# A two-layer hybrid decoder trunk on one core: small opening products and mixer steps queued behind whole projections, band triangles merged, first rows and weights fetched in halves on two queues

## The chip, the core and the metric

The kernel runs on one core of a Trainium2 chip. The metric is the device time of one execution in microseconds. The time before is the median of three runs, 1498.28 us (1497.68 to 1500.63). The profiled execution is a run of its own: it took 1497.97 us, of which the profile's span holds 1496.2 us.

Five engines work from their own instruction lists, each strictly in order: PE (matrix products, with PEld for its weight loads), DVE (vector), ACT (activation), POOL, and SP, which here only issues transfers. A list goes on only when its first instruction has everything that it waits for.

## What is computed

256 rows of 1024 values pass through two layers. Each layer is a half-step feed-forward block (FFN 1), a mixer, and a second feed-forward block (FFN 2). Cut to what matters:

```python
for l in range(DEPTH):                                   # DEPTH = 2
    x = x + 0.5 * rmsnorm(swiglu(rmsnorm(x, g1), w_ffn1_in, w_ffn1_out), ...)
    h = rmsnorm(x, mix_pre_g[l])
    z, xbc, dt, rq, rk, rv, rg, aq, ak, av, gate = split(h @ w_in[l])
    y_ssd = ssd_mixer(z, xbc, dt, ...)                   # chunked scan
    y_ret = retention_mixer(rq, rk, rv, rg, ...)         # chunks of 128
    y_att = swa_sink_attention(aq, ak, av, sinks, band_bias, band_mask)
    y = sum_m(sigmoid(gate_m) * (y_m @ w_branch[m])) @ w_out[l]
    x = x + rmsnorm(y, ...)
    x = x + 0.5 * rmsnorm(swiglu(rmsnorm(x, g2), w_ffn2_in, w_ffn2_out), ...)
```

The attention is causal with a window of 128: a query of the second block of 128 rows sees a triangle of the block before it and the other triangle of its own block, 128 keys in all. There are 16 query heads, 2 key heads, a learned sink per head and a bias that depends on the distance alone.

## The kernel before

All products are made from fp32 values split into a high and a low part (fp32r): `mm3` (L82) issues three matmuls, two on L88 and one on L89, for each slot of 128 input channels. A projection (`gemm`, L96) of one tile t of 128 rows onto 512 columns is 8 slots, 24 matmuls into one PSUM accumulator `acc` (five of these rotate). The FFN out-projection has 22 slots. Weights come as `raw` tiles of 512 KB by SP's queue (`units`, L71; five buffers), are split on ACT (L68, the high part) and DVE (L69, the low part) into `hl`. In the first two chunks of an FFN this is done in halves (128x512).

The rows of x are normalised and transposed by `prenorm` (L173): eight 128x128 transposes on PE (L180), eight scaled copies on ACT (L184, `xT` high), eight on DVE (L188, `xT` low), then two squared sums on ACT (L150). For tile 1 of a stage this is done inside a projection, before slot number `at`.

In an FFN (`ffn`, L336) each projection of a chunk c and a tile t is followed by `swiglu` (L120: Silu on ACT at L125, a product on DVE at L127) and by `transposed` (L155: two transposes of h on PE at L161). In the mixer (`mix`, L739) the key, value and dt columns come first (`kvdt`, 272 columns), followed by `att_kv`, which turns and transposes keys and values (L379, L383). Then eleven projections with their own steps; after each, `pump` (L214) advances the generators of attention, retention and scan by one step each. `finish` runs a generator to its end.

An attention step (`att`, L404) works on four heads and one tile t: scores `pS` on PE (L424), bias and row maximum on DVE (L427), exponentials and the division on ACT (L439, L445), transposes of the probabilities `s` on PE (L451), a copy `pT`, and the product with the values `po` (L459). For t = 1 it keeps 256 score columns per head, of which half are masked, and so has two groups of four transposes.

The order of each engine's list is not the order of the code: a scheduler places the instructions by their dependencies and by the order of the code as priority. `issue_after(i)` in the code adds, for what is written under it, an order behind instruction i on i's own engine; `after` does so for a pair.

The constants of the mixer that no earlier work needs (`mixer_consts`, L727: sink, ea, dsk and dtb as broadcasts of 16 values to 128 partitions, and `cw`, which DVE halves at L737) are placed by the scheduler in the opening of the program, as are the tables of `tables` (L263).

## Time and profile before

| | |
|---|---|
| median of three runs | 1498.28 us |
| the profiled execution | 1497.97 us |
| its span in the profile | 1496.2 us |
| PE busy | 1476.6 us, 99% |
| DVE busy | 996.1 us, 67% |
| ACT busy | 798.4 us, 53% |
| POOL busy | 43.2 us, 3% |
| moved by DMA | 275.28 MB, 184 GB/s in the mean |
| PE in the chain that ended last | 72%, and "issue" 24% |

Busy time of PE holds the pipelined tails of its matmuls, so that one row's end can lie behind the next row's start; the step from one start to the next is what a matmul costs in a full queue. A row of the timeline gives the start, the duration, engine and line, the operation, the tiles, how many equal ones were merged, and in brackets how long the engine stood idle before it and what ended that.

### The profile page before, as it was taken

To read this page: it belongs to the slowest core of one execution; us is meant where nothing else is said; L and a number is where in the kernel's file an instruction comes from. 1 tells how busy PE (TensorE), PEld (TensorE's weight loads), DVE (VectorE), ACT (ScalarE), POOL (GpSimd) and SP (SyncE) were. 2 spreads that over 40 slices of the span, in tenths; PEclk is the share of its full clock that TensorE was granted. 3 is DMA by queue.
4 is the path that set the end of the run, shared out by engine and by line. 5 is a ranking of instruction groups with operands and counts; after the bars stand their busy time and mean duration, and the time that the engine had idled before them with its cause. 6 is when DMAs were issued, how large, how long until landed. Compare 5 with 4: busy or idle time off the path is not lost.

```text
span 1496.2 us, 20006 instructions
## 1 busy us (share of the span) xinstructions
PE 1476.6 (99%) x7277; PEld 1228.2 (82%) x7277; DVE 996.1 (67%) x1647; ACT 798.4 (53%) x1392; POOL 43.2 (3%) x80
## 2 busy tenths in 40 slices
PE   8999999999999999999999999999999999999998
PEld 6888888898888887888878888888888888788886
DVE  6655577688887676655566554777898876755643
ACT  6554466476454456544465454756655544655541
POOL 0000010000100000000000000100001000000000
PEclk9999999999999999999999999999999999999999
DMA  8654456554565545554565544655456645645551
GB/s 302 238 178 169 158 196 208 173 160 152 183 223 185 198 161 194 193 197 153 189 209 186 201 146 172 233 176 163 148 170 200 208 166 176 219 169 173 196 171 66
DMA packets 82771, 275.28 MB, mean 184 GB/s; under 512 B 11120, under 2 KB 15856, under 8 KB 82672
## 3 DMA queue, kind: packets, MB, share of 16 engines
q1 hardware_dynamic: 82384, 273.93, 54.8%
q8 instruction: 57, 0.93, 0.3%
q14 instruction: 42, 0.34, 0.1%
q10 hardware_dynamic: 288, 0.07, 0.0%
HBM read 272.86 MB, written 1.11 MB: 183 GB/s over the span
## 4 chain that ended last, share of the span: by engine, by line
PE 72%; issue 24%; DMA 2%; ACT 1%; POOL 1%; DVE 0%; POOLq 0%; DVEq 0%; ACTq 0%
PE acc L88 39%; PE acc L89 20%; PE xbc L88 3%; PE xbc L89 2%; PE pT L161 1%; PE pS L424 1%; PE py L701 1%; PE po L459 1%; PE pb L451 1%; DMA x<-x 1%; PE po L532 0%; DMA cw<-w_conv 0%; PE pT L180 0%; ACT xT L184 0%; DMA gain<-ffn_post_g 0%
## 5 line engine op out<-in xcount | busy, mean ns | idle before, releaser
L88 PE MATMUL acc<-hl,xT 128*128 128x512 f32 (+1 forms) x2496 | 775.3, 392 | 2.9 <-DVE hl L69 2.9
L69 DVE TENSOR_TENSOR hl<-raw,hl 128x1024 fp32r<-128x1024 f32 (+2 forms) x544 | 592.7, 1108 | 178.5 <-ACT hl L68 160.2
L68 ACT CAST hl<-raw 128x1024 fp32r<-128x1024 f32 (+2 forms) x544 | 510.7, 958 | 239.1 <-PE acc L89 196.3
L88 PEld LDWEIGHTS acc<-hl,xT 128*128 128x128 f32 x2496 | 461.0, 188 | 93.9 <-DVE hl L69 3.6
L89 PE MATMUL acc<-hl,xT 128*128 128x512 f32 (+1 forms) x1248 | 487.2, 392 | 0.0
L89 PEld LDWEIGHTS acc<-hl,xT 128*128 128x128 f32 x1248 | 234.5, 188 | 46.9 <-issue 0.6
L88 PE MATMUL acc<-hl,hT 128*128 128x512 f32 x704 | 216.8, 390 | 0.0
L88 PEld LDWEIGHTS acc<-hl,hT 128*128 128x128 f32 x704 | 131.6, 188 | 26.9
L89 PE MATMUL acc<-hl,hT 128*128 128x512 f32 x352 | 136.4, 389 | 0.0
L127 DVE SCALAR_TENSOR_TENSOR h<-acc,pr,sl 128x256 f32<-128x256 f32 x88 | 42.2, 479 | 119.2 <-ACT sl L125 119.2
L88 PE MATMUL acc<-hl,yT 128*128 128x512 f32 x384 | 120.8, 396 | 0.0
L125 ACT ACTIVATE sl<-acc,pr 128x256 f32<-128x256 f32 x88 | 42.0, 477 | 146.6 <-PE acc L89 146.6
L88 PEld LDWEIGHTS acc<-hl,yT 128*128 128x128 f32 x384 | 71.8, 188 | 16.9 <-issue 2.4
L89 PEld LDWEIGHTS acc<-hl,hT 128*128 128x128 f32 x352 | 66.1, 188 | 13.9
L89 PE MATMUL acc<-hl,yT 128*128 128x512 f32 x192 | 76.1, 396 | 0.0
L88 PE MATMUL xbc<-xT,hl 128*128 128x256 f32 x384 | 72.7, 287 | 0.0
L88 PEld LDWEIGHTS xbc<-xT,hl 128*128 128x128 f32 x384 | 60.4, 191 | 2.2 <-issue 1.5
L166 DVE TENSOR_TENSOR hT<-pT,hT 128x256 fp32r<-128x256 f32 x88 | 37.0, 421 | 30.6 <-ACT hT L164 30.6
L164 ACT CAST hT<-pT 128x256 fp32r<-128x256 f32 x88 | 32.8, 372 | 45.8 <-PE pT L161 45.8
L89 PE MATMUL xbc<-xT,hl 128*128 128x256 f32 x192 | 54.8, 286 | 0.0
L439 ACT ACTIVATE s<-s,nm 128x128 f32<-128x128 f32 (+1 forms) x64 | 28.4, 445 | 34.7 <-DVE nm L433 34.6
L200 DVE TENSOR_TENSOR yg<-acc,gain 128x512 f32<-128x512 f32 x24 | 16.5, 688 | 39.5 <-ACT junk L199 39.5
(189 smaller groups left out, 1149.6 us busy)
## 6 DMA issues: line engine op xcount, KB each, us to landing
raw<-w_ffn_in SPq DMA_DIRECT2D x176, 512.0 KB, 4.8
raw<-w_main SPq DMA_DIRECT2D x152, 512.0 KB, 4.5
raw<-w_ffn_out SPq DMA_DIRECT2D x88, 512.0 KB, 4.6
raw<-w_branch SPq DMA_DIRECT2D x48, 512.0 KB, 4.3
raw<-w_out SPq DMA_DIRECT2D x16, 512.0 KB, 4.5
bias<-rows SPq DMA_DIRECT2D x8, 512.0 KB, 6.3
L<-acs SPq DMA_DIRECT2D x8, 512.0 KB, 5.5
gain<-b_gate SPq DMA_DIRECT2D x6, 512.0 KB, 4.7
```

The costliest lines, as they stand in the source:

```text
L68: nc.scalar.copy(out=hi, in_=src)
L69: nc.vector.tensor_tensor(out=lo, in0=src, in1=hi.bitcast(F32), op=ALU.subtract)
L88: return (mm(ps, xh, wl, start=start, stop=False), mm(ps, xh, wh, start=False, stop=False), mm(ps, xl, wh, start=False, stop=stop))
L89: mm(ps, xl, wh, start=False, stop=stop))
L125: self.last_silu = nc.scalar.activation(out=sl, in_=a, func=AF.Silu, scale=r)
L127: nc.vector.scalar_tensor_tensor(out=h, in0=b, scalar=r, in1=sl, op0=ALU.mult, op1=ALU.mult)
L161: nc.tensor.transpose(ps[:, j], src[:, (q + j) * P:(q + j + 1) * P], self.ident)
L164: nc.scalar.copy(out=d[:, :, 0, ts], in_=p)
L166: nc.vector.tensor_tensor(out=d[:, :, 1, ts], in0=p, in1=d[:, :, 0, ts].bitcast(F32), op=ALU.subtract)
L200: self.nc.vector.tensor_tensor(out=y, in0=ps, in1=g[:, 512 * i:512 * i + 512], op=ALU.mult)
L424: nc.tensor.matmul(pS[:, i, :w], qT[t][:, hb + j + i], kT[:, g, hl, ks], start=hl == 0, stop=hl == 1)
L439: nc.scalar.activation(out=s[:, j], in_=s[:, j], func=AF.Exp, bias=nm[:, j:j + 1], accum_out=l[:, j:j + 1])
```

## The change

Seven edits:

1. In an FFN the two transposes of h of chunks 0 and 1 are held back: they are traced after the next projection and ordered on PE behind its last matmul. In the mixer the same is done for `att_kv` and for `att_q` of the first query projection. The transposes of x for tile 1 move from slot 2 to slot 4 of the second FFN projection, and from slot 5 to slot 7 of the first query projection.
2. `pump` orders what it traces on PE behind the last matmul of the projection before it.
3. Attention for t = 1 keeps 128 score columns per head: a predicated copy on DVE puts the scores of the block before over the masked triangle, the bias is laid out in DRAM as 640 columns per head to match, and the probabilities are transposed once. The values follow as full x v0 + (masked copy) x (v1 - v0), the masked copy `pc` and the difference `vd` being made on DVE.
4. The first rows of x (two halves, SP's queue) and the first weight tile (two halves, ACT's queue) are fetched alternately; the identity is made on POOL instead of fetched.
5. `tables` is ordered on SP behind the last weight fetch issued so far.
6. A Silu of one column on ACT follows the last Tanh of the mixer.
7. A constant `c_prev` is added, `c_ident` dropped.

```diff
     def pump(self):
-        for g in list(self.gens):
-            if next(g, "done") == "done":
-                self.gens.remove(g)
+        with self.tc.issue_after(self.last_mm.ins):
+            for g in list(self.gens):
+                if next(g, "done") == "done":
+                    self.gens.remove(g)
...
         self.x = self.const.tile([P, NT, D], F32, name="x")
-        self.load_x(0)
+        raw = self.rawp.tile([P, 2, 512], F32, tag="raw", name="raw")
+        w = A["w_ffn1_in"][0, 0].rearrange("p (k n) -> p k n", k=2)
+        for i in range(2):
+            nc.sync.dma_start(out=self.x[:, 0, 512 * i:512 * i + 512], in_=A["x"][0, 0:P, 512 * i:512 * i + 512])
+            nc.scalar.dma_start(out=raw[:, i], in_=w[:, i])
+        self.raw0 = raw
...
-        nc.scalar.dma_start(out=ng, in_=A["c_ident"])
+        nc.gpsimd.memset(ng, 1.0)
+        nc.gpsimd.affine_select(out=ng, in_=ng, pattern=[[1, P]], compare_op=ALU.is_equal, fill=0.0, base=0,
+                                channel_multiplier=-1)
...
-        hT, slots = [], {}
+        hT, slots, held = [], {}, []
         order = [(0, 0), (1, 0), (0, 1), (1, 1)] + [(c, t) for c in range(2, NFC) for t in range(NT)]
-        at, where = 2, (1, 0)
+        at, where = 4, (1, 0)
...
             h = self.swiglu(ps[:, 0:256], ps[:, 256:512], r[t])
-            self.transposed(hT[c:c + 1], h, t)
+            if held:
+                with self.tc.issue_after(self.last_mm.ins):
+                    held.pop()()
+            if c < 2:
+                held.append(lambda c=c, h=h, t=t: self.transposed(hT[c:c + 1], h, t))
+            else:
+                self.transposed(hT[c:c + 1], h, t)
             if (c, t) == (2, 1) and self.first:
                 self.first = None
-                self.tables()
+                with self.tc.issue_after(self.fetch.ins):
+                    self.tables()
...
+                    if t:
+                        nc.vector.copy_predicated(out=pS[:, :, :P], data=pS[:, :, P:],
+                                                  mask=self.prev.bitcast(I32).unsqueeze(1).to_broadcast([P, 2, P]))
...
-                pT = []
-                for b in range(t + 1):
-                    pp = self.pbank()
-                    for j in range(4):
-                        nc.tensor.transpose(pp[:, j], s[:, j, b * P:b * P + P], self.ident)
-                    pt = self.t2([4, P], name="pT")
-                    self.copy(pt, pp)
-                    pT.append(pt)
+                pp = self.pbank()
+                for j in range(4):
+                    nc.tensor.transpose(pp[:, j], s[:, j], self.ident)
+                full = self.t2([4, P], name="pT")
+                if t:
+                    nc.scalar.copy(out=full, in_=pp)
+                    cur = self.t2([4, P], name="pc")
+                    nc.vector.tensor_tensor(out=cur, in0=full, in1=self.prev.unsqueeze(1).to_broadcast([P, 4, P]),
+                                            op=ALU.mult)
+                    terms = [(full, vt[:, 0]), (cur, S["vd"])]
+                else:
+                    self.copy(full, pp)
+                    terms = [(full, vt[:, 1])]
...
-            self.att_kv(t, ps)
+            if held:
+                with self.tc.issue_after(self.last_mm.ins):
+                    held.pop()()
+            held.append(lambda: self.att_kv(t, ps))
...
-        main("aq0", 0, s0, 5, self.second)
+        main("aq0", 0, s0, 7, self.second)
...
+        self.after(nc.scalar.activation(out=self.small(1, "w"), in_=self.mhalf, func=AF.Silu), tanh)
```

What the scheduler makes of it is shown at three places. The first is the opening of the program. On DVE there stood before, from the first cast of the identity on (xT is the normalised input, hl the split weights, cw the convolution's weights):

```order
L255 CAST identr<-ng 128x128
L188 SCALAR_TENSOR_TENSOR xT<-pT,pg,xT 128x128 x4
L69 TENSOR_TENSOR hl<-raw,hl 128x512 x2
L188 SCALAR_TENSOR_TENSOR xT<-pT,pg,xT 128x128 x4
L69 TENSOR_TENSOR hl<-raw,hl 128x512 x8
L188 SCALAR_TENSOR_TENSOR xT<-pT,pg,xT 128x128 x8
L69 TENSOR_TENSOR hl<-raw,hl 128x512 x2
L737 TENSOR_SCALAR cw<-cw 128x60
L127 SCALAR_TENSOR_TENSOR h<-acc,pr,sl 128x256
```

and now:

```order
L268 CAST identr<-ng 128x128
L193 SCALAR_TENSOR_TENSOR xT<-pT,pg,xT 128x128 x8
L70 TENSOR_TENSOR hl<-raw,hl 128x512 x8
L770 TENSOR_SCALAR cw<-cw 128x60
L70 TENSOR_TENSOR hl<-raw,hl 128x512 x2
L193 SCALAR_TENSOR_TENSOR xT<-pT,pg,xT 128x128 x8
L70 TENSOR_TENSOR hl<-raw,hl 128x512 x4
L132 SCALAR_TENSOR_TENSOR h<-acc,pr,sl 128x256
```

All eight parts of xT of tile 0 now stand ahead of the first weight split, and cw stands ahead of the low parts of chunk 1's first weights and of tile 1's xT. On ACT, at the same place, before (the first rows issue transfers; junk is the squared sum):

```order
L249 DMA ng<-c_ident 128x128
L303 DMA pg<-ffn_pre_g 128x8
L875 ACT_TABLE_LOAD
L875 ACTIVATE w<-mhalf 128x1
L184 ACTIVATE xT<-pT,pg 128x128 x4
L68 CAST hl<-raw 128x512 x2
L184 ACTIVATE xT<-pT,pg 128x128 x4
L150 ACTIVATE junk,ss<-x 128x512
L68 CAST hl<-raw 128x512 x4
```

and now:

```order
L254 DMA raw<-w_ffn_in 128x512 x2
L319 DMA pg<-ffn_pre_g 128x8
L919 ACT_TABLE_LOAD
L919 ACTIVATE w<-mhalf 128x1
L189 ACTIVATE xT<-pT,pg 128x128 x8
L155 ACTIVATE junk,ss<-x 128x512
L69 CAST hl<-raw 128x512 x6
L155 ACTIVATE junk,ss<-x 128x512
```

The first weight cast moved behind the second four parts of xT and a squared sum, and the gains pg are issued behind two weight halves. The transfers of SP's queue there are now, with nothing of the tables among them:

```order
L253 DMA x<-x 128x512 x2
L79 DMA raw<-w_ffn_in 128x1024 x3
L274 DMA x<-x 128x512 x2
L137 DMA gain<-ffn_post_g 128x1024
L319 DMA pg<-mix_pre_g 128x8
L766 DMA sink<-attn_sinks 128x16
L766 DMA ea<-a_log 128x16
L766 DMA dsk<-d_skip 128x16
L766 DMA dtb<-dt_bias 128x16
L769 DMA cw<-w_conv 128x60
L137 DMA gain<-ret_gn_g 128x1024
```

Between the gain and cw there are only small transfers left; before, c_dmat, c_xi, c_zeta, c_rope and rb stood ahead of the gain, and two weight tiles between the gain and cw.

The second place is PE at the start of FFN 2, behind 30 matmuls of its first two projections before (h is the first product of swiglu, x the rows of tile 1):

```order
L88 MATMUL acc<-hl,xT 128x512 x2
L89 MATMUL acc<-hl,xT 128x512
L161 MATMUL pT<-identr,h 128x128 x2
L180 MATMUL pT<-identr,x 128x128 x8
L88 MATMUL acc<-hl,xT 128x512 x2
```

and now, behind 36 of them, with 12 matmuls between the two kinds of transposes:

```order
L92 MATMUL acc<-hl,xT 128x512
L185 MATMUL pT<-identr,x 128x128 x8
L91 MATMUL acc<-hl,xT 128x512 x2
...
L166 MATMUL pT<-identr,h 128x128 x2
L91 MATMUL acc<-hl,xT 128x512 x4
```

The transposes of h moved behind 18 more matmuls, those of x behind six.

The third place is PE at the last step of attention in a layer (s are the probabilities, pT their transposed copy, po the product with the values, px and rv belong to the scan and to retention). Before, 16 matmuls of the next projection stood between s and po:

```order
L451 MATMUL pb<-identr,s 128x128 x8
L89 MATMUL acc<-hl,xT 128x512
...
L459 MATMUL po<-pT,av 64x256 x4
L650 MATMUL px<-identr,xc 128x128 x4
L532 MATMUL po<-rv,pm 128x256 x2
L88 MATMUL acc<-hl,xT 128x512 x2
```

and now:

```order
L92 MATMUL acc<-hl,xT 128x512
L477 MATMUL pb<-identr,s 128x128 x4
L492 MATMUL po<-pT,av 64x256 x2
L683 MATMUL px<-identr,xc 128x128 x4
L565 MATMUL po<-rv,pm 128x256 x2
L492 MATMUL po<-pc,vd 64x256 x2
L91 MATMUL acc<-hl,xT 128x512 x2
```

The product now stands right behind the transposes whose copy it reads. It is so in both layers at this place; at two others of a layer only a few short products stand between.

More of the change, by code (lines that the diff above doesn't have):

```diff
@@ L74, in units @@
         for h in range(2):
-            raw = self.rawp.tile([P, 2, width], F32, tag="raw", name="raw")
-            nc.sync.dma_start(out=raw, in_=w_ap[2 * u + h].rearrange("p (k n) -> p k n", k=2))
+            raw, self.raw0 = self.raw0, None
+            if raw is None:
+                raw = self.rawp.tile([P, 2, width], F32, tag="raw", name="raw")
+                self.fetch = nc.sync.dma_start(out=raw, in_=w_ap[2 * u + h].rearrange("p (k n) -> p k n", k=2))
             hl = self.hlp.tile([P, 2, 2, width], R, tag="hl", name="hl")
@@ L291, in tables @@
         nc.vector.tensor_tensor(out=rows[:16], in0=ps[:16, :384], in1=nr[:16], op=ALU.add)
-        self.rows = self.dram.tile([16, 384], F32, name="rows")
-        nc.sync.dma_start(out=self.rows, in_=rows[:16])
+        self.rows = self.dram.tile([16, 640], F32, name="rows")
+        nc.sync.dma_start(out=self.rows[:, 0:255], in_=rows[:16, 0:255])
+        nc.sync.dma_start(out=self.rows[:, 384:511], in_=rows[:16, 128:255])
+        nc.sync.dma_start(out=self.rows[:, 511:639], in_=rows[:16, 127:255])
     def const_load(self, n, shape):
@@ L354, in bias_tile @@
         b = self.t4([4, 256], name="bias")
-        src = bass.AP(self.rows.tensor, self.rows.offset + 384 * h0, [[1, P], [384, 4], [1, 256]])
-        self.nc.sync.dma_start(out=b, in_=src)
+        for t in range(NT):
+            src = bass.AP(self.rows.tensor, self.rows.offset + 640 * h0 + 384 * t, [[1, P], [640, 4], [1, P]])
+            self.nc.sync.dma_start(out=b[:, :, t * P:t * P + P], in_=src)
         return b
@@ L408, in att @@
             S["yT2"] = self.new_T(4, "yT")
+            S["vd"] = self.t1([P], name="vd")
+            nc.vector.tensor_tensor(out=S["vd"], in0=vt[:, 1], in1=vt[:, 0], op=ALU.subtract)
         yT = S["yT2"]
@@ L446, in att @@
                 yield
-                pT = []
-                for b in range(t + 1):
-                    pp = self.pbank()
-                    for j in range(4):
-                        nc.tensor.transpose(pp[:, j], s[:, j, b * P:b * P + P], self.ident)
-                    pt = self.t2([4, P], name="pT")
-                    self.copy(pt, pp)
-                    pT.append(pt)
+                pp = self.pbank()
[11 more added lines that the diff above has]
+                    terms = [(full, vt[:, 1])]
                 yield
                 po = self.pst.tile([P, 2, P], F32, tag="pst", name="po")
-                for b in range(t + 1):
+                for b, (p, v) in enumerate(terms):
                     for o in range(2):
-                        nc.tensor.matmul(po[64 * o:64 * o + 64], vt[:, vo + b, 64 * g:64 * g + 64],
-                                         pT[b][:, o::2], start=b == 0, stop=b == t)
+                        nc.tensor.matmul(po[64 * o:64 * o + 64], v[:, 64 * g:64 * g + 64], p[:, o::2],
+                                         start=b == 0, stop=b == t)
                 y = yT[h0 // 4]
@@ L763, in kvdt @@
                                            op0=ALU.mult, op1=ALU.add)
-            self.att_kv(t, ps)
+            if held:
+                with self.tc.issue_after(self.last_mm.ins):
+                    held.pop()()
+            held.append(lambda: self.att_kv(t, ps))
+        held = []
         def main(key, t, slots, at=None, do=None):
@@ L768, in main @@
             n = int(key[2]) if len(key) > 2 else 0
-            if key[:2] == "aq":
+            if held:
+                with self.tc.issue_after(self.last_mm.ins):
+                    held.pop()()
+            if key == "aq0":
+                held.append(lambda: self.att_q(n, t, ps))
+            elif key[:2] == "aq":
                 self.att_q(n, t, ps)
@@ L836, in mix @@
                                                    op0=ALU.mult, op1=ALU.add)
-                    nc.scalar.activation(out=g, in_=g, func=AF.Tanh, scale=0.5)
+                    tanh = nc.scalar.activation(out=g, in_=g, func=AF.Tanh, scale=0.5)
                     self.pump()
@@ L920, in host @@
     out.update(consts())
-    out["c_ident"] = np.eye(P, dtype=np.float32)
     return out
```

12 lines of the change are left out of this document (8 added, 4 removed).

## The prediction

> **What bounds the kernel now.** I read the head of the page first: who is busy.
>
> ```profile
> PE 1476.6 (99%) x7277; PEld 1228.2 (82%) x7277; DVE 996.1 (67%) x1647; ACT 798.4 (53%) x1392; POOL 43.2 (3%) x80
> ```
>
> PE is the bound from end to end. So only two things can shorten the run: matmuls that are not issued, and idle time of PE. Work that moves on DVE or ACT, which are idle for a third and nearly half of the span, counts only where PE comes to wait for it. The next view is therefore the waits of PE alone (us in total, times, longest):
>
> ```profile
> PE pT L161 <- DVE h L127: 6.0, 3, 2.4
> PE acc L88 <- DVE hl L69: 2.9, 1, 2.9
> PE pb L379 <- ACT kh L370: 2.8, 2, 1.4
> PE acc L254 <- DVE warm L251: 1.4, 1, 1.4
> ```
>
> These are all: 13.1 us in seven waits, and no wait at all in the attention, retention and scan steps. The last row is the program's start and stays. The other three are what the change goes for.
>
> **The held products.** Around the longest wait, at the start of FFN 2 of the first layer, the timeline has:
>
> ```profile
> 566.96 0.39 PE L89 MATMUL acc<-hl,xT 128*128 128x512 f32 x1
> 567.63 0.39 PE L89 MATMUL acc<-hl,xT 128*128 128x512 f32 x1
> 568.10 1.28 ACT L125 ACT_TABLE_LOAD   x1 [3.14 <-PE acc L89]
> 569.40 0.47 ACT L125 ACTIVATE sl<-acc,pr 128x256 f32<-128x256 f32 x1
> 569.91 0.49 DVE L127 SCALAR_TENSOR_TENSOR h<-acc,pr,sl 128x256 f32<-128x256 f32 x1 [2.45 <-ACT sl L125]
> 570.45 0.44 PE L161 MATMUL pT<-identr,h 128*128 128x128 f32 x2 [2.42 <-DVE h L127]
> ```
>
> PE's list holds the transposes of h right behind the projection that h comes from, so PE waits out a table load, a Silu and a product. Three matmuls lie between the first two rows, so one is 0.23 us. In the new order 18 more matmuls and the transposes of x stand between, about 5 us, against the 2.42 us of the wait. What is late next would be xT of tile 1, but 12 matmuls follow the transposes of x before it is read: some 2.7 us, and its first part needs one group of ACT copies (1.14 us) and one DVE part behind it. The early Silu takes the table load (1.28 us) to a place where ACT waits anyway; it is worth nothing beyond this, since the wait is already covered. I take the whole 6.0 us; ends are 0 (next paragraphs' rival) and 6.0.
>
> The same at the start of the mixer:
>
> ```profile
> 204.58 1.42 DVE L209 SCALAR_TENSOR_TENSOR x<-yg,r,x 128x512 f32<-128x512 f32 x2 [1.43 <-POOL r L143]
> 205.14 0.39 PE L89 MATMUL acc<-hl,xT 128*128 128x512 f32 x1
> 206.23 0.63 ACT L370 ACTIVATE kh<-acc,pr 128x128 fp32r<-128x128 f32 x2 [3.81 <-DVE dtx L762]
> 206.91 0.33 PE L379 MATMUL pb<-revr,kh 128*128 128x128 f32 x1 [1.38 <-ACT kh L370]
> ```
>
> PE gets six matmuls (1.4 us) and then the transposes of x, whose input is there at 206.0, in place of the wait for kh, which is there at 206.9. Both layers: 2.8 us less. The transposes that follow are now close to the next projection, but the first part of xT's high half stands about 1.3 us behind its transposes, and PE still has three matmuls and four short products (1.1 us) ahead of it; what is left, 0.2 us, I neglect.
>
> **The merged triangles.** Attention for t = 1 issues one group of four transposes where it had two. Four such steps run in each of two layers, so 8 x 4 = 32 transposes go; the products with the values stay the same number. In a full queue eight of them take (a row of the chain):
>
> ```profile
> 286.27 0.87 PE pb L451 x8
> ```
>
> so 0.109 us each and 3.5 us in all, off PE directly. DVE gets 16 predicated copies, 8 products and 2 differences, and loses half the width of 32 reductions; at no more than 0.69 us each (the row of a 128x512 DVE operation below) it is under 18 us on an engine that idles for 500. It costs nothing while the steps keep PE covered.
>
> **Steps behind whole projections.** This is the part with a price. Before, a step's products on PE stood where their inputs were long ready; now at three places of a layer the product with the values follows the transposes of its probabilities at once, or with 0.8 us of other products between. What has to happen in between is one copy:
>
> ```profile
> L68 ACT CAST hl<-raw 128x1024 fp32r<-128x1024 f32 (+2 forms) x544 | 510.7, 958 | 239.1 <-PE acc L89 196.3
> L232 ACT COPY pT<-pb 128x512 f32<-128x512 f32 x12 | 7.0, 585 | 0.8 <-PE pb L451 0.8
> L69 DVE TENSOR_TENSOR hl<-raw,hl 128x512 fp32r<-128x512 f32 x112 | 70.7, 686 | 44.6 <-ACT hl L68 43.8
> ```
>
> A last transpose ends about 0.25 us after its start, the copy takes 0.585 us and a hand-over some 0.05 us on either side: 0.9 us. With nothing between, that is 0.9 us of idle PE; with 0.8 us between, 0.1 us; and where the masked copy on DVE (0.69 us by the third row) comes behind it, about 0.3 us more at one place. 1.4 us a layer, 2.8 us in all. The lower end is 0. The upper end: at each of the six places the copy stands behind a weight cast on ACT, 0.96 us each by the first row, so 2.8 + 5.8 = 8.6 us. I take 2.8, since ACT is busy only half of the time.
>
> **The opening.** Here the trace speaks against the change. The rows:
>
> ```profile
> 4.59 1.38 PE L180 MATMUL pT<-identr,x 128*128 128x128 f32 x8
> 5.57 1.14 ACT L184 ACTIVATE xT<-pT,pg 128x128 fp32r<-128x128 f32 x4 [2.44 <-PE pT L180]
> 7.50 1.14 ACT L68 CAST hl<-raw 128x512 fp32r<-128x512 f32 x2 [0.79 <-DMA raw<-w_ffn_in]
> 8.15 1.29 DVE L69 TENSOR_TENSOR hl<-raw,hl 128x512 fp32r<-128x512 f32 x2 [0.28 <-ACT hl L68]
> 8.90 1.22 PE L88 MATMUL acc<-hl,xT 128*128 128x512 f32 x2 [2.93 <-DVE hl L69]
> 9.56 0.64 ACT L150 ACTIVATE junk<-x 128x512 bf16<-128x512 f32 x1
> 10.08 0.21 ACT L150 ACTIVATION_READ_ACCUMULATOR junk<-x 128x1 f32 x1
> 15.05 2.17 ACT L184 ACTIVATE xT<-pT,pg 128x128 fp32r<-128x128 f32 x8
> 16.93 1.07 PE L88 MATMUL acc<-hl,xT 128*128 128x512 f32 x4
> ```
>
> The first matmul waits for the first weights, which land at 7.5 us. With halves they land earlier, but that is not what PE will wait for: ACT's new list has all eight parts of xT (2.17 us) and one squared sum (0.64 + 0.21 us) ahead of the first weight cast (0.57 us), and DVE's low part (0.64 us) comes behind that. And xT needs the gains pg, which are now issued behind two weight halves on ACT's queue. The windows of the opening (two last columns: share of the DMA engines' time, GB/s; before them the granted clock of PE):
>
> ```profile
> 2.00:4.00 2.00, 2.00 (x6) 1.58 (x5) 0.00 (x0) 1.12 (x2) 0.00 (x0) 1.00 0.83 282
> 4.00:6.00 2.00, 1.97 (x10) 1.39 (x9) 0.23 (x1) 0.43 (x2) 0.00 (x0) 1.00 0.92 249
> 8.00:10.00 2.00, 1.10 (x3) 0.91 (x4) 1.58 (x4) 2.00 (x7) 0.00 (x0) 0.67 1.02 412
> 10.00:12.00 2.00, 2.00 (x6) 1.33 (x5) 2.00 (x6) 2.00 (x6) 0.00 (x0) 0.50 1.06 413
> 12.00:14.00 2.00, 2.00 (x10) 1.55 (x10) 1.81 (x4) 2.00 (x5) 0.84 (x2) 0.97 1.04 383
> ```
>
> The four halves are 1.05 MB; the first 6 us moved 1.06 MB, so pg is there at about 6.2 us and no earlier than 5.57. The first matmul then starts at 6.2 + 2.17 + 0.85 + 0.57 + 0.64 + 0.2 for hand-overs = 10.6 us, 1.7 later than now (1.1 later with pg at 5.57).
>
> The clock columns say that PE ran at half clock for about 3.5 us after its idle 2.9 us. The gap grows to some 5 us, so I keep these 3.5 us as they are. The Trainium skill, TensorE: Matmul & The Clock Gate, "What's actually happening", says that the clock drops after an idle window of about 3.4 us and comes back after as long a busy one; by it the sum would be the same, unless the gap were cut short, which is part of the first rival. The Trainium skill, DMA: Bandwidth & Descriptors, "Issuing engines are not separate DMA queues", says that transfers issued by several engines share the same 16 DMA engines and interleave; the share of 1.02 to 1.06 at 412 GB/s agrees, and by it the two queues bring the sum of the four halves no earlier.
>
> A second thing decides the opening, and comes later. The new list of DVE holds cw ahead of the low parts of chunk 1's first weights and of xT of tile 1. Before, these stood ahead of it. The chain has:
>
> ```profile
> 12.04 5.18 DMA gain<-ffn_post_g
> 17.24 6.57 DMA cw<-w_conv
> ```
>
> so the gain landed at 17.22 us and cw at 23.81 us, 6.59 us later, with two weight tiles and five small transfers between (DVE even waited 3.06 us for it, at no cost to PE). Ahead of the gain there go now:
>
> ```profile
> c_dmat<-c_dmat SPq DMA_DIRECT2D x1, 256.0 KB, 8.7
> c_xi<-c_xi SPq DMA_DIRECT2D x1, 256.0 KB, 7.9
> c_rope<-c_rope SPq DMA_DIRECT2D x1, 192.0 KB, 5.8
> ng<-c_ident ACTq DMA_DIRECT2D x1, 64.0 KB, 3.4
> ```
>
> 768 KB, 1.9 us at 412 GB/s: the gain lands at 15.3 us. Two weight tiles of 512 KB are 2.5 us, so the small transfers cost 6.59 - 2.5 = 4.1 us, and cw lands at 19.4 us. DVE then needs about 0.2 us for cw and 0.64 us for the first low part, and PE can start its 27th matmul (chunk 1 with tile 0) at 20.3 us. Now, PE starts its 25th at 16.93 us and its 27th 0.46 us later, at 17.4. So PE is 2.9 us late here. From the first matmul alone it would be 1.7 us late; the two do not add, the later one counts. Ends: 1.1 us, if cw is early and pg as now; and with the four broadcasts twice as slow, 2.9 + 4.1 = 7.0 us. Weights are no bound behind this: 34 matmuls (7.8 us) of chunk 0 and of what has landed stand ahead of the next tile's.
>
> POOL's fill and selection for the identity have no row of their own; a mean POOL instruction takes 43.2 / 80 = 0.54 us, and from the program's start to the transposes at 4.59 us two of them have room for four times that. I take nothing; were they slower than this, the opening would move by the excess, one for one, and no reason speaks for a gain.
>
> **The sum.** -6.0 - 2.8 - 3.5 + 2.8 + 2.9 = -6.6 us on the profiled execution's 1497.97, so 1491.4; the median of the runs is 0.3 us above that execution, so 1491.7 us for the median.
>
> **Rivals.** First, the opening gains as its edits say: the first matmul no longer waits (2.9 us), and neither cw nor pg is late. Then -6.0 - 2.8 - 3.5 + 2.8 - 2.9 = -12.4 us, 1485.9 us. For it: the weights do land first at 7.5 us. Against it: the order of ACT and DVE above. 0.15.
>
> Second, cw is the later end: the opening loses 7.0 us, the sum is -2.5 us, and the time 1495.8, hardly measurable. For it: the chain ran through cw even before. Half of the way to it is as likely as the end itself. 0.12.
>
> Third, the waits only move: the held products wait where they are now (their inputs come later too, because steps bunch on DVE), and only the transposes are saved. -3.5 + 2.8 + 2.9 = +2.2 us: 1500.5 us, no change. Against it: 5 us of cover against 2.42. 0.08.
>
> Fourth, on the other side: slower. With each step's products bunched behind a projection, PE waits at most pumps and not at six places, for a copy of the kind above with no cover, 0.9 us. A layer has about 20 pumps between the first attention step and the last; 40 x 0.9 = 36 us in place of 2.8, so +26.6 us and 1524.9 us. It decides from 14 such waits on: 14 x 0.9 = 12.6 us against the 9.4 us that the rest gains and the 3 us that can be measured. For it: DVE is the busiest helper in these stretches, and five accumulators give it only so much lag. Against it: in the new order only three places of a layer have so little cover. 0.05.
>
> The forecast itself gets 0.60. A difference of 0.2%, 3 us, is about what a measurement of this kernel can tell from no change. Below 1495.3 lie the forecast, the first rival and half of the second: 0.60 + 0.15 + 0.06 = 0.81; within 0.2% the other half of the second and the third, 0.14; slower the fourth, 0.05. The range holds the forecast with the bounds of its two unknown costs on the steps and in the opening, not both at their worst, and reaches to the first two rivals: 1485.0 to 1497.0 us.
>
> **What would show it.** In the new profile: no wait of PE for h or kh; 64 transposes in the group of s in place of 96; the first matmul of a projection at 10 to 11 us, behind a squared sum on ACT; DVE idle before cw until about 19 us, and PE idle until about 20; waits of PE for pT at three places of a layer, a microsecond or less each. I am wrong in the opening if the first matmul stands before 8.9 us or the 27th before 17.4; wrong on the steps if PE's waits for copies exceed 8.6 us; wrong on the gain if the rows for h or kh are still there.

## The result and the profile after

The changed kernel takes 1507.86 us (median of four runs, 1507.58 to 1508.1), the kernel before 1498.93 us (four runs). The ratio is 1.0059, 95% interval 1.0041 to 1.0076: slower by about 9 us. The prediction was 1491.7 us with a range up to 1497.0; it had the wrong sign and missed by 16 us. Of all executions timed here one, of own_slots below, ran slow (2599.94 us at a mean granted clock of 0.67); without it the median of that run is 1489.93 us and not 1489.98.

The profiled execution took 1508.1 us, its span is 1506.4 us, 10.2 more than before. The busy row of PE and the waits of PE (engine, line, what it waited for: us in total, times, longest) answer to the first two views of the prediction:

```profile
PE 1480.7 (98%) x7245; PEld 1228.7 (82%) x7245; DVE 993.8 (66%) x1665; ACT 792.5 (53%) x1394; POOL 42.2 (3%) x82
```

```profile
PE acc L91 <- DVE hl L70: 5.6, 1, 5.6
PE po L492 <- DVE pc L482: 4.2, 2, 2.1
PE acc L91 <- DVE gz L595: 3.2, 2, 1.8
PE pb L477 <- ACT s L473: 1.8, 3, 0.8
PE acc L91 <- DVE rv L821: 1.7, 2, 0.8
PE acc L267 <- DVE warm L264: 1.5, 1, 1.5
PE po L492 <- ACT pT L480: 1.3, 2, 0.7
```

The rows for h and kh are gone, as forecast. In their place stand five rows of the mixer, 12.2 us. PE's busy time rose by 4.1 us though it has 32 matmuls fewer: part of them ran at half clock.

Where the time went is read by setting the start of the same product on PE side by side in the two traces (us). Edit 1 moves the transposes of x against the matmuls around them, so the start of a mixer is read behind them, at a matmul of the query projection of tile 1 (L89 before, L92 now) ahead of which both lists hold the same products:

| product on PE | before | after | after - before |
|---|---|---|---|
| first of the out-projection of FFN 1, layer 0 | 137.87 | 141.27 | +3.40 |
| in the query projection of tile 1, mixer 0 | 228.16 | 229.78 | +1.62 |
| first of the second branch, layer 0 | 466.23 | 475.84 | +9.61 |
| first of the out-projection of FFN 2, layer 0 | 689.57 | 696.55 | +6.98 |
| first of the out-projection of FFN 1, layer 1 | 877.84 | 883.45 | +5.61 |
| in the query projection of tile 1, mixer 1 | 968.12 | 971.97 | +3.85 |
| first of the second branch, layer 1 | 1206.14 | 1219.20 | +13.06 |
| first of the out-projection of FFN 2, layer 1 | 1429.54 | 1439.91 | +10.37 |

So the opening cost 3.4 us; the held transposes of h gave 2.6 + 1.4 + 2.7 = 6.7 us back (the early Silu lies in the same stretches); each start of a mixer gave 1.8 us; and the stretch from there to the second branch cost 8.0 us in the first layer and 9.2 us in the second. The last two numbers are the surprise.

The opening in the timeline of the changed kernel:

```profile
8.47 2.18 ACT L189 ACTIVATE xT<-pT,pg 128x128 fp32r<-128x128 f32 x8 [4.78 <-DMA pg<-ffn_pre_g]
...
11.10 3.25 ACT L69 CAST hl<-raw 128x512 fp32r<-128x512 f32 x6
...
12.54 1.22 PE L91 MATMUL acc<-hl,xT 128*128 128x512 f32 x2 [5.62 <-DVE hl L70]
...
16.73 0.19 DVE L770 TENSOR_SCALAR cw<-cw 128x60 f32<-128x60 f32 x1
```

The order of ACT is the one that the prediction showed; but pg lands at 8.4 us, not 6.2, so the first projection starts at 12.54 us and not at 10.6. cw has no idle time in brackets: nothing waited for it.

The end of attention in the first layer, in the timeline of the changed kernel (ACT, DVE and PE):

```profile
340.57 0.59 ACT L238 COPY pT<-pb 128x512 f32<-128x512 f32 x1 [1.21 <-PE pb L477]
341.06 0.69 ACT L594 ACTIVATE gz<-acc,rh 128x512 f32<-128x512 f32 x1
...
360.61 0.59 ACT L480 COPY pT<-pb 128x512 f32<-128x512 f32 x1 [0.30 <-PE pb L477]
...
361.15 2.36 DVE L70 TENSOR_TENSOR hl<-raw,hl 128x1024 fp32r<-128x1024 f32 x2
...
362.04 0.69 ACT L594 ACTIVATE gz<-acc,rh 128x512 f32<-128x512 f32 x1
...
363.82 0.69 DVE L482 TENSOR_TENSOR pc<-pT,c_prev 128x512 f32<-128x512 f32 x1
364.56 1.12 PE L492 MATMUL po<-pc,vd 128*64 128x256 f32 x4 [2.08 <-DVE pc L482]
366.29 0.68 DVE L595 SCALAR_TENSOR_TENSOR gz<-gz,acc 128x512 f32<-128x512 f32 x1
367.03 1.22 PE L91 MATMUL acc<-hl,xT 128*128 128x512 f32 x2 [1.34 <-DVE gz L595]
```

gz (`silu2`, L590 of the changed kernel) is what reads a gate projection out of its accumulator, first on ACT (L594), then on DVE (L595). There is one for each tile of 128 rows. On ACT the first runs at 341 us, the second 21 us later, each close behind a copy pT of an attention step. PE first waits for the masked copy pc, and then for the accumulator that the second gz still holds. The same stretch of the timeline before has the two together:

```profile
343.12 0.59 ACT L232 COPY pT<-pb 128x512 f32<-128x512 f32 x1 [0.21 <-PE pb L451]
343.61 1.27 ACT L561 ACTIVATE gz<-acc,rh 128x512 f32<-128x512 f32 x2
```

And the waits bring the clock down. The windows of PE there (window, PE busy and instructions, granted clock, share of the DMA engines, GB/s):

```profile
361.00:364.00 3.00, 1.48 (x9) 1.00 0.69 209
364.00:367.00 3.00, 1.12 (x4) 0.58 0.87 288
367.00:370.00 3.00, 2.97 (x7) 0.50 0.64 195
370.00:373.00 3.00, 3.00 (x12) 0.78 0.02 7
```

From 367.03 to about 371.3 us PE runs at half clock, which costs 2.1 us, and 0.5 us more on the four products at 364.56 (1.12 us in place of 0.65). In the second layer, by the same rows, it is 2.8 us. Waits of 12.2 us and 5.4 us of half clock are 17.6 us, against the 17.2 us by which the two stretches grew.

### The profile page after: what moved, and what is told of

Same layout as the page of the kernel before. It is cut to its first block, busy times and chain, and to the rows that moved or that the text cites. A ratio compares the mean times of both kernels' runs of the same rounds, so it can differ in the third digit from the quotient of the medians.

```text
span 1506.4 us, 20004 instructions
## 1 busy us (share of the span) xinstructions
PE 1480.7 (98%) x7245; PEld 1228.7 (82%) x7245; DVE 993.8 (66%) x1665; ACT 792.5 (53%) x1394; POOL 42.2 (3%) x82
## 4 chain that ended last, share of the span: by engine, by line
PE 85%; issue 12%; DVE 1%; ACT 0%; DMA 0%; POOL 0%; ACTq 0%; DVEq 0%; POOLq 0%
PE acc L91 48%; PE acc L92 24%; PE xbc L91 3%; PE pT L166 2%; PE xbc L92 2%; PE pS L449 1%; PE py L734 1%; PE po L492 1%; PE pT L185 1%; PE pb L477 1%; DVE hl L70 0%; DMA pg<-ffn_pre_g 0%; PE po L565 0%; PE pb L422 0%; PE px L683 0%
## 5 line engine op out<-in xcount | busy, mean ns | idle before, releaser
L91 PE MATMUL acc<-hl,xT 128*128 128x512 f32 (+1 forms) x2496 | 778.0, 393 | 10.4 <-DVE hl L70 5.6
L92 PE MATMUL acc<-hl,xT 128*128 128x512 f32 (+1 forms) x1248 | 488.9, 393 | 0.0
L92 PEld LDWEIGHTS acc<-hl,xT 128*128 128x128 f32 x1248 | 235.6, 189 | 47.2 <-issue 0.6
L92 PE MATMUL acc<-hl,hT 128*128 128x512 f32 x352 | 136.4, 389 | 0.0
L91 PEld LDWEIGHTS acc<-hl,yT 128*128 128x128 f32 x384 | 71.8, 188 | 17.1 <-issue 2.9
L92 PEld LDWEIGHTS acc<-hl,hT 128*128 128x128 f32 x352 | 66.1, 188 | 13.8
L92 PE MATMUL acc<-hl,yT 128*128 128x512 f32 x192 | 75.7, 394 | 0.0
L92 PE MATMUL xbc<-xT,hl 128*128 128x256 f32 x192 | 54.6, 285 | 0.0
L92 PEld LDWEIGHTS acc<-hl,yT 128*128 128x128 f32 x192 | 36.1, 188 | 7.3
```

Source lines behind the costliest of these rows:

```text
L91: return (mm(ps, xh, wl, start=start, stop=False), mm(ps, xh, wh, start=False, stop=False), mm(ps, xl, wh, start=False, stop=stop))
L92: mm(ps, xl, wh, start=False, stop=stop))
```

## The experiments

Each was timed in five rounds beside the kernel before (its medians were 1500.4 to 1501.0 us in these groups). The changed kernel was not timed again there, so a difference to its 1507.86 us is one between groups, in which the kernel before lay 1.5 to 2.1 us apart. The table has all runs; the ratio is to the kernel before, with its 95% interval. Edits 5 and 6 were not undone by themselves, and what each is worth stays open.

| run | median us | ratio |
|---|---|---|
| bands_apart | 1506.19 | 1.0039 (1.0027 to 1.0052) |
| mix_unheld | 1492.34 | 0.9950 (0.9937 to 0.9962) |
| unheld_apart | 1495.13 | 0.9966 (0.9952 to 0.9979) |
| old_fetch | 1504.84 | 1.0028 (1.0017 to 1.0039) |
| q_now | 1491.16 | 0.9938 (0.9924 to 0.9952) |
| kv_now | 1508.74 | 1.0056 (1.0042 to 1.0069) |
| unheld_old_fetch | 1490.36 | 0.9932 (0.9919 to 0.9945) |
| pg_first | 1504.97 | 1.0027 (1.0015 to 1.0038) |
| catch_up | 1507.29 | 1.0045 (1.0031 to 1.0060) |
| late_start | 1493.31 | 0.9955 (0.9942 to 0.9968) |
| pc_pool | 1506.22 | 1.0041 (1.0028 to 1.0054) |
| q_now_old_fetch | 1488.23 | 0.9921 (0.9907 to 0.9936) |
| own_slots | 1489.98 | 0.9928 (0.9916 to 0.9940) |
| own_catch_up | 1497.36 | 0.9977 (0.9968 to 0.9985) |
| own_old_fetch | 1487.37 | 0.9913 (0.9900 to 0.9927) |
| own_q_now_old_fetch | 1486.59 | 0.9909 (0.9895 to 0.9923) |

One suspect needed no run. With the `issue_after` in `pump` (edit 2) taken out, the lists of all five engines come out the same, instruction by instruction. And with all the other edits undone and edit 2 kept, the lists are those of the kernel before. Edit 2 moves nothing; what the prediction put down to it is the work of another edit.

**Which edit: the merge or the held products?** Two edits, undone one by one and together.

bands_apart puts `bias_tile`, `rows` and `att` back as they were:

```diff
-                pp = self.pbank()
-                for j in range(4):
-                    nc.tensor.transpose(pp[:, j], s[:, j], self.ident)
+                for b in range(t + 1):
+                    pp = self.pbank()
+                    for j in range(4):
+                        nc.tensor.transpose(pp[:, j], s[:, j, b * P:b * P + P], self.ident)
```

> The changed kernel with edit 3 undone: attention for t = 1 again keeps 256 columns, two groups of transposes, no masked copy pc. Held products and all else stay. Theory H (the held products of the mixer push attention one projection later, so that its last steps stand with little cover between transposes and product, whatever the products are): the transposes come back (+3.5 us), the waits for pc go (4.2 us and what follows on them, at most 8 us), waits for pT of the other kind come in their place; 1503 to 1511 us. Theory M (the masked copy on DVE and the added DVE work of the merge cost the time, in any order): 1507.9 + 3.5 - 18.7 = 1492.7 us, and no PE waits for pT above 1 us in all.

mix_unheld leaves the merge and undoes the mixer's part of edit 1:

```diff
-            held.append(lambda: self.att_kv(t, ps))
+            self.att_kv(t, ps)
...
-            if key == "aq0":
-                held.append(lambda: self.att_q(n, t, ps))
-            elif key[:2] == "aq":
+            if key[:2] == "aq":
...
-        main("aq0", 0, s0, 7, self.second)
+        main("aq0", 0, s0, 5, self.second)
```

> The changed kernel with the mixer's part of edit 1 undone: att_kv and att_q are traced at once again, the transposes of x stand before slot 5 of the first query projection. The merge of the triangles and the held transposes of the FFNs stay. Theory H: between the transposes of s and the product that reads their copy there are 3.5 us of other matmuls or more, so no PE waits for po, s, gz, rv; kh waits return (at most 2.8 us): 1507.9 - 18.7 + 1.5 to 2.8 = 1490.7 to 1492 us. Theory M: pc still stands behind weight splits on DVE, PE waits for it: 1505 to 1510 us.

unheld_apart has both diffs.

> Both undone: the mixer's held products and the merge. What stays of the change are the opening, the held transposes of the FFNs, the early Silu, the order of the tables. Theory H: mix_unheld plus 32 transposes of 0.109 us: 1494 to 1495.5 us. Theory M: the same as bands_apart, 1492.7 us or a little above by the waits for kh. Against the kernel before both say: + 3.4 (opening) - 6.7 (waits for h) = -3.3 us.

Without the merge: 1506.19 us. Without the held products: 1492.34 us. The waits of PE in mix_unheld are

```profile
PE acc L91 <- DVE hl L70: 5.7, 1, 5.7
PE pb L403 <- ACT kh L394: 2.8, 2, 1.4
PE acc L267 <- DVE warm L264: 1.5, 1, 1.5
```

and nothing else of note: no pc, gz, s or rv. The masked copy is there in the same number, on the same engine, and PE never waits for it. Theory M falls; the loss belongs to the held products of the mixer. unheld_apart at 1495.13 shows what the merge is worth: 2.8 us in the medians, of which 1.1 us are a difference of the two openings in the traces, so nearer to 2. Beside the held products it is worth nothing: bands_apart, without the merge, took 1506.19 us and the changed kernel 1507.86.

**Which held product?** q_now and kv_now each undo one half.

```diff
-            if key == "aq0":
-                held.append(lambda: self.att_q(n, t, ps))
-            elif key[:2] == "aq":
+            if key[:2] == "aq":
```

> The changed kernel with one thing of edit 1 undone: att_q of the first query projection is traced at once; att_kv stays held, the transposes of x stay before slot 7. Theory Hq (holding att_q lets attention start one pump later, so that its last steps meet the end of the projections; this is the cost): one place per layer with no cover between transposes and product is left, 0.74 us each, the others go and with them the half clock; no kh wait either: 1490.5 to 1492.5 us. Theory Hkv (holding att_kv, which makes keys and values late, is the cost) or slot 7: it stays at 1505 to 1510 us.

```diff
-            if held:
-                with self.tc.issue_after(self.last_mm.ins):
-                    held.pop()()
-            held.append(lambda: self.att_kv(t, ps))
+            self.att_kv(t, ps)
```

> The reverse: att_kv is traced at once, att_q of the first query projection stays held, slot 7 stays. Theory Hq: all waits at the end of attention stay (pc 2.1 us, gz 1.7 us, s 0.8 us, rv 0.8 us a layer and the half clock), and waits for kh can come back: 1507.5 to 1510 us. Theory Hkv: 1491 to 1494 us.

1491.16 and 1508.74 us: holding att_q is the whole of it. In q_now one wait of the five is left,

```profile
PE po L492 <- ACT pT L480: 1.4, 2, 0.7
```

the one place where the product stands right behind its transposes, and it costs what the prediction had worked out for such a place (0.7 us against 0.9).

**Why? First answer: attention is one pump late.** With att_q held, the first attention generator finds its queries one projection later. catch_up gives the step back; late_start makes q_now late in the same way.

```diff
+            if key == "aq1" and not t:
+                next(att[0])
             self.pump()
```

> The changed kernel, att_q still held, and one step of attention more: at the pump behind the first aq1 projection the first attention generator is advanced twice, so that it is level with the kernel in which att_q is not held. Theory Hq (the one pump that attention starts late is the cost): the waits for pc, gz, s and rv go, one wait of 0.7 us for pT per layer stays, 1490.5 to 1492.5 us. If the held products themselves (their place on PE, or what they delay on DVE and ACT) cost it: 1505 to 1510 us.

```diff
         while f"aq{g}1" not in S:
             yield "wait"
+        if g == 0:
+            yield "wait"
```

> The kernel with att_q traced at once (q_now), but the first attention generator lets one pump pass before its first step. The last steps then have 2.2 to 4.8 us of other matmuls between transposes and product, not 0.0 to 1.0 as in the changed kernel. If a late start alone brings the loss: 1503 to 1510 us. If the loss needs the little cover that the last steps have in the changed kernel's list: PE waits for gz or pc for less than 3 us in all, 1490.5 to 1495 us.

Both went against it. catch_up stayed at 1507.29 us; its waits at the end of attention are gone but for 1.3 us for pT, but PE now waits earlier, about 265 to 290 us, for rb, the rotation's second tile:

```profile
PE acc L91 <- DVE rb L512: 5.0, 2, 2.5
PE xbc L91 <- DVE rb L512: 4.8, 3, 2.5
```

late_start took 1493.31 us, 2 us more than q_now, with small waits:

```profile
PE po L494 <- DVE pc L484: 1.4, 2, 0.7
PE pb L479 <- ACT s L475: 0.7, 2, 0.3
```

Lateness alone is worth 2 us. The theory falls; the other answer that late_start allowed, that the loss needs the little cover of the changed kernel's last steps, stands so far.

**Is it DVE's list?** pc stands behind two weight splits of 1.2 us each on DVE. pc_pool moves it to POOL.

```diff
-                    nc.vector.tensor_tensor(out=cur, in0=full, in1=self.prev.unsqueeze(1).to_broadcast([P, 4, P]),
+                    nc.gpsimd.tensor_tensor(out=cur, in0=full, in1=self.prev.unsqueeze(1).to_broadcast([P, 4, P]),
```

> The changed kernel with the masked copy pc made by POOL, which is idle there, and not by DVE. Theory Q (PE waits because pc stands behind two weight splits in DVE's list): the wait for pc goes or falls under 0.5 us a layer, and with it the clock's drop; 1500 to 1503 us. Theory B (the whole list of DVE is late there, pc only the first that PE meets): PE then waits for gz, which frees the accumulator, until about the same time; DVE has 0.7 us less to do at each place, 1505.5 to 1507.5 us.

1506.22 us. The wait for pc fell from 4.2 to 2.6 us, and the wait for gz grew from 3.2 to 6.6:

```profile
PE acc L91 <- DVE gz L595: 6.6, 2, 3.3
...
PE po L492 <- POOL pc L482: 2.6, 2, 1.3
```

pc is only the first late thing that PE meets. Behind it stands the accumulator that gz has not emptied. Theory B has the number right, and its reason, that the whole list of DVE is late there, is part of it: in the changed kernel gz is late on ACT first (362.04 us), though ACT is idle for 47% of the span, and its second half on DVE comes another 4.3 us later (366.29 us), at the end of a stretch in which DVE has not waited since 357.87 us.

**What gz waits for: a buffer.** gz, rb, pT and pc are all tiles of `t2`, one set of ten buffers. In the compiled program of both kernels all 139 tiles of t2 are first written in the order of the code, without one exception. So gz of tile 1, which the code has behind an attention step, should get no buffer before that step's pT and pc have theirs, and these come only when the step's transposes are done. Until then the projection's accumulator stays full, and PE has five of them. own_slots gives pT and pc three buffers of their own and leaves seven to t2; nothing else of the code is touched.

```diff
-N4, N2, N1 = 17, 10, 6
+N4, N2, N1 = 17, 7, 6
...
-                full = self.t2([4, P], name="pT")
+                full = self.big.tile([P, 4, P], F32, tag="pp", name="pT", bufs=3)
...
-                    cur = self.t2([4, P], name="pc")
+                    cur = self.big.tile([P, 4, P], F32, tag="pp", name="pc", bufs=3)
```

> The changed kernel, all edits kept, but the transposed probabilities pT and their masked copy pc have three buffers of their own; the shared buffers t2 go from ten to seven. Theory F (buffers of t2 are given out in the order of the code: the tanh of a gate projection, gz, can't have one before the attention step written ahead of it has had its own for pT and pc, so an accumulator stays full until the step's transposes are done; with att_q held the steps are late and this falls on rg0 of tile 1): gz of tile 1 stands right behind that of tile 0 on ACT, no PE wait for gz, pc under 1 us a layer, 1490 to 1495 us. Theory L (the steps of attention are late and DVE has too much to do at the end, whatever the buffers): 1503 to 1510 us.

1489.98 us: 17.9 us less than the changed kernel (19.7 us by the two ratios), with every edit kept and the same memory. These are all waits of PE that are left:

```profile
PE acc L91 <- DVE hl L70: 5.8, 1, 5.8
PE acc L267 <- DVE warm L264: 1.5, 1, 1.5
```

and on ACT gz no longer stands behind a pT:

```profile
329.61 0.67 ACT L594 ACTIVATE gz<-acc,rh 128x512 f32<-128x512 f32 x1
...
334.77 0.59 ACT L238 COPY pT<-pb 128x512 f32<-128x512 f32 x1 [0.20 <-PE pb L477]
...
340.06 0.67 ACT L594 ACTIVATE gz<-acc,rh 128x512 f32<-128x512 f32 x1
```

The first gz runs 11.5 us earlier than in the changed kernel, the second 22 us earlier. That the two would stand together, as expected, did not come true: they run about 4 and 9 us behind the last matmuls of their projections, where it was about 16 and 31 us, and the second one's half on DVE follows 1.6 us behind its half on ACT, not 4.3. Theory L falls: the crowd on DVE goes with the shared buffers. One thing is not separated by this run. The lists of PE, ACT and DVE come out in another order with it, and the products of the layer's last two steps now start 5.4 and 6.5 us behind their last transpose, where in the changed kernel they start 1.5 and 1.0 us behind it. So the shared set is shown as the cause of the loss; how much of it went because the accumulators come free, and how much because the last products have cover again, is not shown. Nor was one larger shared set tried. The same buffers in catch_up:

> The kernel with att_q held and one step of attention more (catch_up, 1507.3 us, in which PE waited 9.8 us for rb of the rotation), with the same buffers of their own for pT and pc. Theory F: rb took its buffer behind pT of a step ahead of it in the code; the waits for rb go, 1490 to 1494 us. If the extra step crowds DVE there whatever the buffers: 1503 to 1508 us.

1497.36 us: 10 us better, but 3 us short of the expectation. The waits at the end stay away; 7.0 us of waits for rb remain in six places (9.8 in five without). Whether seven shared buffers are too few there or the extra step crowds DVE wasn't tried and stays open.

**The opening.** old_fetch undoes edit 4 alone; pg_first keeps it and only issues the gains ahead of the weight halves on ACT's queue.

```diff
-        for i in range(2):
-            nc.sync.dma_start(out=self.x[:, 0, 512 * i:512 * i + 512], in_=A["x"][0, 0:P, 512 * i:512 * i + 512])
-            nc.scalar.dma_start(out=raw[:, i], in_=w[:, i])
-        self.raw0 = raw
+        self.load_x(0)
+        self.raw0 = None
...
-        nc.gpsimd.memset(ng, 1.0)
-        nc.gpsimd.affine_select(out=ng, in_=ng, pattern=[[1, P]], compare_op=ALU.is_equal, fill=0.0, base=0,
-                                channel_multiplier=-1)
+        nc.scalar.dma_start(out=ng, in_=A["c_ident"])
```

> The changed kernel with edit 4 undone: x and the first weight tile are fetched whole tile by tile on SP's queue, the identity comes by DMA on ACT's queue ahead of the gains pg. Everything behind the opening keeps its order on PE. If the opening's loss comes from pg (issued behind two weight halves, landing at 8.4 us) and its half clock, the first projection's matmul is back at about 8.9 us and the time is 1507.9 - 3.4 = 1504.5 us. If cw ahead of the low parts decides the opening, as the prediction had it, PE still waits there at about 17 to 20 us and the time stays within 1 us of 1507.9.

```diff
+        self.pg0 = self.sm.tile([P, KD], F32, tag="pg", name="pg", bufs=2)
+        nc.scalar.dma_start(out=self.pg0, in_=A["ffn1_pre_g"][0])
         for i in range(2):
```

> The changed kernel with the gains pg issued on ACT's queue ahead of the two weight halves and not behind them; the list of ACT then has four parts of xT, four weight casts and only then the other four parts. PE's list is the same but for two rows. Theory P (the opening lost by pg, which landed at 8.4 us behind a whole weight tile): pg lands by 3 us, xT starts at about 5.7 us, weights are there at 5.2 and 6.4 us, the first matmul of a projection starts at 8.0 to 8.5 us, and 1507.9 - 4 = 1504 us. Theory C (cw ahead of the low parts decides, as the prediction had it): the first matmul is early but PE idles later, 1506 to 1508 us.

1504.84 and 1504.97 us: 3 us each by the medians (3.4 and 4.3 us by the spans of the traces), and as much by moving one transfer of 4 KB as by undoing the whole edit. The DMA issues (KB each, us from issue to landing) of pg in the changed kernel and in pg_first:

```profile
pg<-ffn_pre_g ACTq DMA_DIRECT2D x1, 4.0 KB, 6.7
```

```profile
pg<-ffn_pre_g ACTq DMA_DIRECT2D x1, 4.0 KB, 3.5
```

It landed at 8.4 us there and at 4.2 us here, later than the 3 us expected. In pg_first the first projection starts at 8.71 us, 0.2 us before the kernel before; it then waits once more, since the second weight half lands only at 8.3 us, and runs at half clock:

```profile
8.71 0.74 PE L91 MATMUL acc<-hl,xT 128*128 128x512 f32 x2 [2.14 <-DVE hl L70]
...
10.51 1.14 PE L91 MATMUL acc<-hl,xT 128*128 128x512 f32 x2 [0.83 <-DVE hl L70]
```

cw lands at 18.7 us in it, and between 18 and 20 us PE waits 0.4 us for a low part that stands behind cw on DVE: theory C fits pg_first in small, and the changed kernel not at all.

**The versions that beat both.**

> The mixer's part of edit 1 and edit 4 undone together: merge, held transposes of the FFNs, early Silu and the order of the tables stay. If the two costs are apart in time and add: 1492.3 - 3.0 = 1489.3 us. If the opening's loss is made up later (PE runs into the same late thing in both): 1491 to 1492.3 us.

> The version that the runs so far point to: of the changed kernel everything but the holding of att_q and the fetches in halves (edit 4). q_now took 1491.2 us and the old fetches gave 2 us beside the unheld mixer and 3 us alone: 1488.2 to 1489.2 us, faster than both kernels; at 1491 or above the two gains would not add.

> own_slots with the fetches of before (edit 4 undone). Theory F: 3 us below own_slots, 1487 to 1492 us: with buffers of their own all of the held products can stay. Theory L: 1500 to 1507 us.

> q_now_old_fetch (1488.2 us), the best so far, with the buffers of their own: between transposes and product there are now 3 us of other matmuls or more everywhere, so the wait for pT of 0.7 us a layer goes: 1486.5 to 1487.5 us; if seven shared buffers are too few for the rest, slower than 1488.2.

They took 1490.36, 1488.23, 1487.37 and 1486.59 us; the second and the last as expected, the first 1 us above (the old fetches gave 2.0 us there and not 3.0), own_old_fetch within its range. The last differs from the third in att_q traced at once; between these two the intervals don't decide. Its waits of PE:

```profile
PE acc L91 <- DVE hl L70: 2.6, 1, 2.6
PE acc L261 <- DVE warm L258: 1.4, 1, 1.4
PE pT L166 <- DVE h L132: 0.5, 1, 0.5
```

## Why the prediction was wrong, step by step

**The held products of the FFNs: right.** Forecast -6.0 us, measured -6.7 by the table of starts.

**The start of the mixer: right.** The rows for kh are gone, and PE gained 1.8 us each, 3.5 in all, for a forecast of 2.8. The 0.7 us more were not followed up.

**The merged triangles: right in sign, too large.** 32 transposes at 0.109 us were to give 3.5 us. mix_unheld against unheld_apart gives 2.0 us in the same stretches of the traces (1.0 a layer) and 2.8 us in the medians. The prediction added this to the other terms; beside the held products it did not come (1506.19 us without the merge).

**Steps behind whole projections: this step failed.** Forecast +2.8 us with 8.6 as the upper end; measured some 17 to 19 us, of which the traces show 17.6: 7.3 us of waits for s, pT and pc, 4.9 us of waits for accumulators (gz and rv), and 5.4 us of half clock behind them. The prediction looked at three places where a product stands behind its own transposes, and costed one copy there. Such a place does cost 0.7 us, as q_now shows. It took the masked copy for 0.3 us more at one place; PE waited 2.1 us a layer for it, behind two weight splits of DVE. The waits for accumulators and the half clock have no term in it at all. Behind both lies the shared set of buffers, in which a reader's buffer is kept back for an attention step ahead of it in the code: with other buffers for pT and pc all these waits go, and the half clock with them (own_slots). The prediction asked of each moved instruction what it reads, and not what it needs to write to. It also gave the move to the wrong edit: it took `issue_after` in `pump` for the cause, which moves nothing. Held att_q does it.

**The opening: nearly right in size, wrong in the path.** Forecast +2.9 us, measured +3.4. The prediction let cw decide (19.4 us) and put the first projection at 10.6 us; it started at 12.54 us, cw was there at 15.9 us by the trace of transfers, and nothing waited for it. The four small broadcasts ahead of cw, costed at 4.1 us, landed 0.2 to 0.5 us apart. What was late was pg: the bytes of the four halves had been counted, but not the weight tile that was issued on the other queue at the same moment. The Trainium skill, DMA: Bandwidth & Descriptors, "Issuing engines are not separate DMA queues", says that transfers of several issuing engines interleave on the same 16 engines; the trace agrees, pg landing 0.6 us behind that 512 KB tile (8.4 and 7.8 us), and the prediction cited the rule and didn't apply it to pg. The rows that it set beside the rule, 8 to 14 us, hold transfers of SP's queue alone: they show full engines, not two queues that share them.

**The rivals.** The fourth had the side, but its place and price were others: it saw a copy of 0.9 us without cover at most pumps, 14 of them to turn the sign. There were eleven waits in the mixers, of 12.2 us, close to the 12.6 us that it needed to turn the sign, and 4.9 us of them were for accumulators. Its condition, "for it: DVE is the busiest helper, and five accumulators give it only so much lag", named the resource and then priced another. That was worth more than 0.05.

The sum with the measured terms: -6.7 - 3.5 - 2.0 + 19.2 + 3.4 = +10.4 us against the 10.2 us that the span grew, the fourth term being the two mixers' 8.0 + 9.2 us with the transposes' 2.0 put back. It adds up by the way it is read; that 2.0 us were saved beside the held products too is not shown.

## What to carry to other kernels

Where a scheduler hands out shared buffers in the order of the code, moving a step moves what everything behind it may write to: look for the operation that empties an accumulator, and for what stands ahead of it in the code with a tile of the same set. Here tiles that wait for a long chain (pT, pc) and tiles that free the bound engine (gz, rb) were better not in one set: splitting ten buffers into seven and three was worth 17.9 us on the changed kernel, twice what the change had lost. On q_now_old_fetch, where att_q is not held, it gave 1.6 us by the medians, which the intervals do not tell from nothing; on the kernel before it was not tried. And before an edit is given a price, see that undoing it alone changes the lists.

## What the runs showed of the hardware

The prediction counted half clock in the opening alone; the clock fell in the mixers too, after shorter gaps. In the first layer of the changed kernel the four products behind a wait of 2.08 us ran at half clock (1.12 us against 0.65). In the second layer as long a wait left them at 0.65 us, and what stands behind the next wait ran at half clock:

```profile
1107.28 0.65 PE L492 MATMUL po<-pc,vd 128*64 128x256 f32 x4 [2.08 <-DVE pc L482]
1109.74 1.22 PE L91 MATMUL acc<-hl,xT 128*128 128x512 f32 x2 [1.81 <-DVE gz L595]
```

In pg_first, 2.14 us idle, 1.0 us of work and 0.83 us idle were enough:

```profile
8.00:10.00 2.00, 0.98 (x3) 1.00 1.03 410
10.00:12.00 2.00, 1.49 (x4) 0.66 1.05 414
```

In the kernel before, a single wait of 2.42 us in front of 570.45 us left the clock alone:

```profile
570.00:572.00 2.00, 1.55 (x12) 1.00 0.04 16
```

So no single length of a gap decides. The Trainium skill, TensorE: Matmul & The Clock Gate, "What's actually happening", speaks of an idle window of about 3.4 us on a grid that runs freely. That the grid runs freely fits the unequal cases. Read as a window that is idle throughout, the rule does not fit, since PE worked within any 3.4 us ahead of the drop at 364.56 us.
